# Attention scores with a head's two query parts in the two partition halves, and a new sequence of the mixer's steps, in a hybrid decoder layer

## The chip, the cores and the metric

The kernel runs on one core of one Trainium2 chip. The metric is the device time of one execution in microseconds. A core has five engines that each work through a fixed list of instructions in order and wait for each other through semaphores: TensorE (PE in the profile, its weight loads PEld), VectorE (DVE), ScalarE (ACT), GpSimd (POOL) and SyncE (SP), which issues the transfers from memory.

## The reference

One decoder layer on 512 tokens of width 1024, in float32. Three parts follow each other: a SwiGLU half-step (inner width 2816), a token mixer, a second SwiGLU half-step with a gated embedding behind it. The change is inside the mixer, in the attention scores:

```python
z = h @ w_in[i]
zq, zk, zv, zc, zg = [z[..., offs[j]:offs[j + 1]] for j in range(len(SPLIT_SIZES))]
q = rmsnorm(zq.reshape(B, S, N_Q_HEADS, HEAD_DIM), q_norm[i])
k = rmsnorm(zk.reshape(B, S, N_KV_HEADS, HEAD_DIM), k_norm[i])
q = partial_rope(q, cos, sin)
k = partial_rope(k, cos, sin)
a = sliding_window_attention(q, k, v, sinks[i]) @ attn_proj[i]
...
s = jnp.einsum('bnqhgd,bnkhd->bnhgqk', qb, kb, preferred_element_type=jnp.float32) * scale
valid = (delta >= 0) & (delta < WINDOW) & (kpos >= 0)
...
merged = jax.nn.sigmoid(ga) * a + jax.nn.sigmoid(gb) * c
x = x + merged @ w_out[i]
```

There are 16 query heads and 2 key heads of 64 channels, and 8 query heads share a key head. Tokens stand in 4 blocks of 128. The queries of a block see the keys of their own block and of the block before; block 0 has no block before it. Beside the attention (a) the mixer has a convolution branch (c): a gated projection, a causal depthwise convolution with 31 taps over 1024 channels, a layer norm, a projection. Two further projections (ga, gb) gate the two branches.

## The kernel before, in words

**Number format.** Every large product is done with operands in a rounded float32 format (F32R). To keep the precision, an operand x is split into a high part xh = round(x), written by ScalarE, and a low part xl = x - xh, written by DVE (`split_into`, L681). A product of two split operands is three products: wh·xl, wl·xh, wh·xh (`mm3`, L708). All weights are split in this way as they arrive, in pieces of 128x1024: the transfer fills raw, ScalarE writes whi, DVE or POOL writes wlo (the remainder).

**What sets the order of the work.** The code does not issue instructions directly. `record` (L652) records every operation with its operands; a planner (`simulate`, `plan`) plays the five engines through with a cost for each operation, and gives each operation an engine slot and each tile a buffer. The order on PE begins with the sequence in which groups of products were recorded; a group whose inputs are late may be overtaken by up to nine others, and five passes feed the result back. On the other engines the operation with the earliest due time goes first. Remainders of some weights are "flex": the planner puts them on DVE or on POOL. The finished lists are fixed in the program. PSUM gives 8 buffers.

**The mixer's steps.** `ORDER` (L40) is a string that gives the sequence in which the mixer's steps are recorded: K (keys and values), Q0, Q1 (queries of head groups 0 and 1), a0 to a7 and b0 to b7 (the two halves of the convolution's gated projection, for eight channel blocks; the convolution of a channel block follows its b step), A, E and V (scores, softmax, values; A0 to A3 are group 0 and blocks 0 to 3, A4 to A7 group 1), g and h (the gates ga and gb), p (the attention's output projection), L (the convolution's layer norm), e (the embedding's product). After them come the convolution's projection (cp) and the output (wo).

**Scores.** `scores(g, t)` (L1259) handles the eight heads of group g in token block t as four pairs j. In the tiles a pair lies in the partitions: head j, which uses key head 0, in partitions 0 to 63, and head j + 8, which uses key head 1, in 64 to 127. PE transposes the queries (qTp), they are split into qT_h and qT_l with all 128 partitions, and `mm3` multiplies them with kz. The tile kz (high and low) holds for key head 0 the keys in partitions 0 to 63 and zeros in the others, for key head 1 the other way round; so one product with both key heads side by side gives both heads of the pair. Per pair there are three products of 512 columns (two key heads, two blocks of 128 keys), or of 256 columns in block 0. Four POOL memsets write the zeros.

**Around it.** Behind the scores ScalarE copies the part of the own block, DVE puts in the earlier block by a predicated copy, finds the maximum, and ScalarE takes the exponentials. `values(g, t)` (L1314) transposes the probabilities (pT), splits them (p_h, p_l) and multiplies them with the values (o). `conv(c)` (L1133) runs the taps of five channel blocks on DVE (tiles cz, 29 steps each) and of three on ScalarE (ct) and POOL (y).

Of the kernel before, what the change touches and what calls it, by code (L numbers as in the profile page):

```python
# [9 lines left out]
F32 = mybir.dt.float32  # L10
F32R = mybir.dt.float32r
I32 = mybir.dt.int32
AF = mybir.ActivationFunctionType
ALU = mybir.AluOpType
AX = mybir.AxisListType

P = 128
# [8 lines left out]
HD = 64  # L26
NPAIR = NH // 2
W = 128
# [9 lines left out]


ORDER = """  # L40
K0 a0 b0 a1 Q0 A0 b1 a3 a2 A1 b2 E0 E1 b3 A2 E2 a4 V0 A3 a5 E3 V1 b4 Q1 V2 b5
V3 A5 a7 A6 g5 h7 A4 E5 A7 E6 E4 V6 g3 a6 E7 g0 V5 b6 V4 g4 g6 V7 h1 g2 h4 b7
g1 p0 p2 g7 p3 L0 p4 h3 p7 h2 p5 p1 e0 e1 p6 h5 h0 h6
"""
POOLCH = (0, 2, 4)
WARM = 9
# [605 lines left out]
def record():  # L652
    nc = Program()

    def ps_tile(name):
        return nc.tile(name, [P, S], F32, "ps")
# [4 lines left out]
    def rtile(name):  # L661
        return nc.tile(name, [P, S], F32R, "a")

    def small(name, n):
        return nc.tile(name, [P, n], F32, "c")
# [15 lines left out]
    def split_into(hi, lo, src, scale=None, eng=nc.vector):  # L681
        if scale is None:
            nc.scalar.activation(hi, src, AF.Copy)
            eng.tensor_tensor(lo, src, hi.bitcast(F32), op=ALU.subtract)
        else:
            nc.scalar.activation(hi, src, AF.Copy, scale=scale)
            nc.vector.scalar_tensor_tensor(
                lo, src, scale, hi.bitcast(F32), op0=ALU.mult, op1=ALU.subtract
            )

    def split(name, src, scale=None):
        hi, lo = rtile(f"{name}_h"), rtile(f"{name}_l")
        split_into(hi, lo, src, scale)
        return hi, lo
# [13 lines left out]
    def mm3(ps, w, x, start, stop, first=1, skip=False):  # L708

        nc.tensor.matmul(ps, w[first], x[0], start=start, stop=False, skip_group_check=skip)  # L710
        nc.tensor.matmul(ps, w[1 - first], x[0], start=False, stop=False, skip_group_check=skip)
        nc.tensor.matmul(ps, w[0], x[1], start=False, stop=stop, skip_group_check=skip)
# [132 lines left out]
    x, h = [], []  # L845
# [248 lines left out]
    def next_norm(tag, gain):  # L1094
        h, ss = [], SumSq(f"{tag}_ss")

        def after(o):
            h.append(split(f"{tag}_h{o}", x[o], gain[:, o : o + 1]))
            ss.in_psum(x[o], KD)

        return h, ss, after

    h2, ss2, after = next_norm("mix", g_mix)
# [92 lines left out]


    kz = [nc.tile(f"kz{p}", [P, NKV, S], F32R, "k") for p in "hl"]
    for z in kz:
        nc.behind = next(o for o in reversed(nc.ops) if o.eng == "PE")  # L1200
        nc.gpsimd.memset(z.bitcast(F32)[HD:P, 0], 0.0)
        nc.gpsimd.memset(z.bitcast(F32)[0:HD, 1], 0.0)
        nc.behind = None


    vd = [nc.tile(f"v{t}", [P, 2, NKV, 2, HD], F32R, "a") for t in range(NT)]
# [3 lines left out]
    def keys_values():  # L1210
        pss = token_major("kv", "wkv", 0, 2, 4, 2 * P)
        norm2()
        k3s = []
        for t in range(NT):
            z = nc.tile(f"zk{t}", [P, NKV, HD], F32, "a")
            p4 = pss[t].rearrange("p (b d) -> p b d", d=HD)
            r = r2k[:, t : t + 1]
            nc.scalar.activation(z, p4[:, 0:2], AF.Copy, scale=r)
            nc.scalar.activation(vf[:, t], p4[:, 2:4], AF.Copy, scale=r)
            for hh in range(NKV):  # L1220
                split_into(vp[t][:, hh, hh], vp[t][:, hh, 1 - hh], p4[:, 2 + hh], scale=r)
            k3s.append(z)
        for t in range(NT - 1, 0, -1):
            nc.gpsimd.tensor_tensor(vf[:, t], vf[:, t], vf[:, t - 1], op=ALU.subtract)
            for hh in range(NKV):
                split_into(dv[t][:, hh, hh], dv[t][:, hh, 1 - hh], vf[:, t, hh], eng=nc.gpsimd)
        rk = heads_rsqrt("k", k3s, NKV, 1.0, True)
        for t, k3 in enumerate(k3s):
            nc.vector.tensor_tensor(k3, k3, rk[t].unsqueeze(2).broadcast_to([P, NKV, HD]), op=ALU.mult)
            rest = k3[:, :, 16:HD]  # L1230
            nc.gpsimd.tensor_tensor(rest, rest, gqk.unsqueeze(1).broadcast_to([P, NKV, HD - 16]), op=ALU.mult)
            rope(f"k{t}", k3, NKV, kcs, t)
        pt = ps_tile("kTp")
        with nc.group("kT"):
            for t, k3 in enumerate(k3s):
                nc.tensor.transpose(pt[:, t * P : (t + 1) * P], k3.rearrange("p h d -> p (h d)"), ident)
        halves = [slice(hh * HD, (hh + 1) * HD) for hh in range(2)]
        for hh in range(2):
            r = halves[hh]
            split_into(kz[0][r, hh], kz[1][r, hh], pt[r])  # L1240

    zq, rq = {}, {}

# [15 lines left out]
    def scores(g, t):  # L1259

        pt = ps_tile(f"qTp{g}_{t}")
        with nc.group(f"qT{g}_{t}"):
            for j in range(4):
                nc.tensor.transpose(pt[:, j * P : (j + 1) * P], zq[g, t][:, j * P : (j + 1) * P], ident)
        qT = split(f"qT{g}_{t}", pt)
        nb = 1 if t == 0 else 2  # L1270
        t0 = t + 1 - nb
        s = [nc.tile(f"s{g}_{t}_{i}", [P, 2, 2, W], F32, "a") for i in range(2)]
        m = small(f"m{g}_{t}", 8)
        for j in range(4):
            ps = ps_tile(f"sc{g}_{t}_{j}")
            ps4 = ps.rearrange("p (h c k) -> p h c k", h=2, c=2)
            with nc.group(f"sc{g}_{t}_{j}"):
                q = [qT[i][:, j * P : (j + 1) * P] for i in range(2)]
                kk = [kz[i][:, :, t0 * W : (t + 1) * W] for i in range(2)]
                mm3(ps4[:, :, 0:nb], q, kk, True, True)  # L1280
            sj = s[j // 2][:, j % 2]
            if t == 0:
                nc.vector.tensor_tensor(sj, ps4[:, :, 0], later, op=ALU.add)
            else:
                nc.scalar.copy(sj, ps4[:, :, 1])
                nc.vector.copy_predicated(sj, later.bitcast(I32), ps4[:, :, 0])
            if j % 2:
                mj = m[:, 2 * j - 2 : 2 * j + 2].rearrange("p (j h) -> p j h", h=2)
                nc.vector.tensor_reduce(mj, s[j // 2], axis=AX.X, op=ALU.max, negate=True)
        nc.vector.tensor_tensor(m, m, rq[g][t], op=ALU.mult)  # L1290
        nc.vector.tensor_tensor(m, m, sinks_n[:, 8 * g : 8 * g + 8], op=ALU.min)
        state[g, t] = s, m
# [68 lines left out]
    def norm2():  # L1361
        nonlocal rb2, r2k
        rr = mean_rstd("mix_n", ss2.accs, D)
        r2k = rr[1]
        rb2 = spread("mix_n", rr)
# [102 lines left out]
    h3, ss3, after = next_norm("f2", g_ffn2)  # L1468
    for o in range(KD):
        ps = proj(f"wo{o}", "wout", o, mg)  # L1470
# [4 lines left out]
    h4, ss4, after4 = next_norm("pg", g_gate)  # L1475
# [4 lines left out]
    for o in range(KD):  # L1480
        ps = proj(f"pg{o}", "wgate", o, h4)
# [140 lines left out]
```

## Time and profile before

| | |
|---|---|
| median of 3 runs | 1172.97 us (1172.74 to 1175.81) |
| profiled execution | 1174.18 us, span of the trace 1172.4 us |
| PE busy | 1161.6 us (99%), 6740 products |
| DVE busy | 973.4 us (83%) |
| ScalarE busy | 639.7 us (55%) |
| POOL busy | 456.2 us (39%) |
| mixer: first key product, first cp, first wo product | 354.0, 690.3, 733.8 us |
| score products | start from 422.8 to 533.5 us, 96 of them |

Tiles are named as in the program: ca and cb are the products of the steps a and b, sc the scores, o the values, q0b and q1b the query projections, wlo_... the weight remainders, sg the convolution's sigmoid gate, u its input, sga and sgb the gates, ln_... the convolution's layer norm, ple_... the embedding's norm. The whole program is issued by a helper, so nearly all rows carry line 1522, and operations are told apart by tile. A product's duration runs from its start to its modelled end, and products overlap; the rate is read from the starts.

### The profile page before, as it was taken

The page shows a single profiled execution, that of the slowest core. Times are in us where ns is not written, and L with a number is a line of the kernel's source. Part 1 is how long each engine was busy: PE and PEld are TensorE (multiplying, and loading weights), DVE is VectorE, ACT ScalarE, POOL GpSimd, SP SyncE. Part 2 cuts the span into 40 slices and gives each one's busy share as a digit, 9 for nine tenths or more (in the row PEclk, how much of TensorE's full clock was granted, in tenths as well). Part 3 has the DMA queues.
Part 4 walks back from the last instruction along what each step waited for, and adds up shares of the span by engine and source line. Part 5 has one row for each costly group of instructions (what it writes and reads, how often), then busy time and mean ns, then how long its engine had stood idle before and what let it go on. Part 6 is the DMA issues. An engine that isn't in the chain of part 4 may idle for free.

```text
span 1172.4 us, 17962 instructions
## 1 busy us (share of the span) xinstructions
PE 1161.6 (99%) x6740; PEld 1029.6 (88%) x6740; DVE 973.4 (83%) x1481; ACT 639.7 (55%) x1139; POOL 456.2 (39%) x418
## 2 busy tenths in 40 slices
PE   9999999999999999999999999999999999999998
PEld 7898899889988888878888888889988999899886
DVE  8995799679886898999999786678966997599885
ACT  8552455335545579979865573545541555245542
POOL 2430465033303987887898600104402440122000
PEclk9999999999999999999999999999999999999999
DMA  7422323342233221312223233332333223331331
GB/s 226 146 85 96 126 75 106 99 136 76 82 104 100 90 91 37 108 55 72 76 89 106 88 94 93 105 96 102 107 104 132 74 86 100 121 127 41 104 108 72
DMA packets 37815, 115.30 MB, mean 98 GB/s; under 512 B 4704, under 2 KB 9440, under 8 KB 37728
## 3 DMA queue, kind: packets, MB, share of 16 engines
q1 hardware_dynamic: 37584, 114.12, 31.0%
q8 instruction: 53, 0.87, 0.3%
q14 instruction: 34, 0.28, 0.1%
q10 hardware_dynamic: 144, 0.03, 0.0%
HBM read 112.04 MB, written 2.10 MB: 97 GB/s over the span
## 4 chain that ended last, share of the span: by engine, by line
PE 94%; ACT 2%; DVE 2%; POOL 1%; issue 1%; DMA 0%; SPq 0%; DVEq 0%; ACTq 0%
PE f_d L1522 20%; PE ap L1522 4%; PE ga L1522 4%; PE pg L1522 4%; PE cp L1522 4%; PE wo L1522 4%; PE ca L1522 3%; PE gb L1522 3%; PE cb L1522 3%; PE f_u L1522 2%; PE f_g L1522 2%; PE q1b L1522 2%; PE q0b L1522 2%; PE sc L1522 2%; PE f_u14b L1522 1%; PE f_u20b L1522 1%
## 5 line engine op out<-in xcount | busy, mean ns | idle before, releaser
L1522 POOL TENSOR_TENSOR f_s<-raw_wgu,raw_wgu 128x512 f32<-128x512 f32 x51 | 86.6, 1710 | 345.5 <-DMA raw_wgu<-in_wgu 115.6
L1522 POOL TENSOR_TENSOR y<-y,ct 128x507 f32<-128x507 f32 (+27 forms) x90 | 119.1, 1343 | 6.2 <-ACT ct L1522 4.6
L1522 ACT ACTIVATE whi_wgu<-raw_wgu 128x1024 fp32r<-128x1024 f32 (+1 forms) x93 | 76.2, 834 | 81.5 <-PE f_d L1522 29.5
L1522 DVE TENSOR_TENSOR wlo_wgu<-raw_wgu,whi_wgu 128x1024 fp32r<-128x1024 f32 (+1 forms) x93 | 105.1, 1140 | 7.8 <-ACT whi_wgu L1522 7.3
L1522 DVE SCALAR_TENSOR_TENSOR cz<-u,dww,cz 128x504 f32<-128x504 f32 (+25 forms) x145 | 104.7, 732 | 2.3
L1522 ACT ACTIVATE whi_wd<-raw_wd 128x1024 fp32r<-128x1024 f32 (+1 forms) x48 | 47.4, 987 | 103.9 <-PE f_d L1522 84.6
L1522 DVE TENSOR_TENSOR f_d<-f_d,f_n_rb 128x512 f32<-128x512 f32 x48 | 33.4, 697 | 75.8 <-PE f_d L1522 75.8
L1522 DVE TENSOR_TENSOR f_wl<-f_s,f_wh 128x512 fp32r<-128x512 f32 x72 | 71.4, 1012 | 1.5 <-ACT f_wh L1522 1.0
L1522 POOL TENSOR_TENSOR f_s<-raw_wgu,f_s 128x512 f32<-128x512 f32 x31 | 52.3, 1694 | 51.6 <-DVE f_us L1522 20.6
L1522 DVE TENSOR_TENSOR wlo_wgu<-f_s,whi_wgu 128x512 fp32r<-128x512 f32 x80 | 66.3, 863 | 6.0 <-ACT whi_wgu L1522 5.8
L1522 ACT ACTIVATE whi_wgu<-f_s 128x512 fp32r<-128x512 f32 x80 | 46.6, 625 | 32.4 <-PE f_d L1522 8.9
L1522 ACT ACTIVATE ct<-u,dww 128x505 f32<-128x505 f32 (+28 forms) x90 | 58.2, 701 | 2.2 <-DVE u L1522 2.1
L1522 ACT ACTIVATE f_wh<-f_s 128x512 fp32r<-128x512 f32 x72 | 43.6, 626 | 26.6 <-DVE f_s L1522 12.9
L1522 POOL TENSOR_TENSOR f_s<-f_s,raw_wgu 128x512 f32<-128x512 f32 x31 | 49.2, 1594 | 20.8 <-DVE f_s L1522 6.0
L1522 DVE TENSOR_TENSOR wlo_wd<-raw_wd,whi_wd 128x1024 fp32r<-128x1024 f32 (+1 forms) x48 | 54.1, 1128 | 3.8 <-ACT whi_wd L1522 3.6
L1522 ACT ACTIVATE f_gs<-f_gs 128x512 f32<-128x512 f32 x44 | 27.6, 629 | 34.8 <-DVE f_gs L1522 34.4
L1522 POOL TENSOR_TENSOR f_t<-x 128x256 f32<-128x256 f32 x8 | 6.5, 807 | 86.8 <-DVE x L1522 81.6
L1522 DVE SCALAR_TENSOR_TENSOR x<-f_d,x 128x512 f32<-128x512 f32 x48 | 32.9, 689 | 1.4
L1522 DVE TENSOR_TENSOR f_s<-raw_wgu,raw_wgu 128x512 f32<-128x512 f32 x25 | 32.9, 1319 | 0.0
L1522 ACT ACTIVATE s<-s,m,q_r 128x128 f32<-128x128 f32 x64 | 31.0, 491 | 0.5 <-DVE m L1522 0.4
L1522 ACT ACTIVATE whi_wzc<-raw_wzc 128x1024 fp32r<-128x1024 f32 x16 | 17.0, 1061 | 22.3 <-issue 8.4
L1522 ACT ACTIVATE whi_wzg<-raw_wzg 128x1024 fp32r<-128x1024 f32 x16 | 17.1, 1069 | 16.9 <-PE ga L1522 5.0
(1621 smaller groups left out, 4525.3 us busy)
## 6 DMA issues: line engine op xcount, KB each, us to landing
raw_wgu<-in_wgu SPq DMA_DIRECT2D x80, 512.0 KB, 3.7
raw_wd<-in_wd SPq DMA_DIRECT2D x32, 512.0 KB, 3.5
raw_wzc<-in_wzc SPq DMA_DIRECT2D x16, 512.0 KB, 3.6
raw_wzg<-in_wzg SPq DMA_DIRECT2D x16, 512.0 KB, 3.6
raw_wd<-in_wd SPq DMA_DIRECT2D x16, 384.0 KB, 3.1
raw_wgu<-in_wgu SPq DMA_DIRECT2D x32, 128.0 KB, 2.9
raw_wq<-in_wq SPq DMA_DIRECT2D x8, 512.0 KB, 3.6
raw_wap<-in_wap SPq DMA_DIRECT2D x8, 512.0 KB, 3.6
```

The costliest lines, as they stand in the source:

```text
L1522: getattr(engines[op.eng], op.what)(*a, **k)
```

## The change

In `scores` the split of the transposed queries is laid out in another way. For head hh of a pair there is one tile qT[hh]: in the head's own 64 partitions the high part, in the other 64 the low part of the same head. kz now holds, for each key head, the same keys in both halves. A product of qT[hh] with the high keys so gives (qh + ql)·kh, and a second one with the low keys gives (qh + ql)·kl. Per pair that is four products, two for each head, of 256 columns, or of 128 in block 0. The zeros and their memsets are gone; the keys take four ScalarE and four DVE instructions on 64 partitions for two and two; the queries of a step take two ScalarE and two DVE instructions on 64 partitions and 512 columns for one and one on 128 partitions. `ORDER` has the same steps in another sequence.

```diff
 ORDER = """
-K0 a0 b0 a1 Q0 A0 b1 a3 a2 A1 b2 E0 E1 b3 A2 E2 a4 V0 A3 a5 E3 V1 b4 Q1 V2 b5
-V3 A5 a7 A6 g5 h7 A4 E5 A7 E6 E4 V6 g3 a6 E7 g0 V5 b6 V4 g4 g6 V7 h1 g2 h4 b7
-g1 p0 p2 g7 p3 L0 p4 h3 p7 h2 p5 p1 e0 e1 p6 h5 h0 h6
+K0 a0 a1 b0 Q0 A0 a3 b1 E0 a2 A1 E1 b3 a5 A2 V1 a4 E2 b2 V0 A3 E3 b4 Q1 V2 A6
+h7 V3 E6 b5 a7 A5 g5 A4 E5 E4 A7 V5 V6 g3 g6 a6 b6 h1 V4 g4 E7 b7 g0 V7 h3 h4
+p0 g2 g1 h2 g7 p2 p3 h6 p5 p6 p1 L0 p4 h5 e0 e1 h0 p7
 """
...
     kz = [nc.tile(f"kz{p}", [P, NKV, S], F32R, "k") for p in "hl"]
-    for z in kz:
-        nc.behind = next(o for o in reversed(nc.ops) if o.eng == "PE")
-        nc.gpsimd.memset(z.bitcast(F32)[HD:P, 0], 0.0)
-        nc.gpsimd.memset(z.bitcast(F32)[0:HD, 1], 0.0)
-        nc.behind = None
+    mixer = next(o for o in reversed(nc.ops) if o.eng == "PE")
...
         for hh in range(2):
             r = halves[hh]
-            split_into(kz[0][r, hh], kz[1][r, hh], pt[r])
+            nc.behind = mixer
+            for to in (r, halves[1 - hh]):
+                nc.scalar.activation(kz[0][to, hh], pt[r], AF.Copy)
+            for to in (r, halves[1 - hh]):
+                nc.vector.tensor_tensor(kz[1][to, hh], pt[r], kz[0][r, hh].bitcast(F32), op=ALU.subtract)
+            nc.behind = None
...
-        qT = split(f"qT{g}_{t}", pt)
+
+        qT = [rtile(f"qT{g}_{t}_{hh}") for hh in range(2)]
+        for hh in range(2):
+            r, other = (slice(h * HD, (h + 1) * HD) for h in (hh, 1 - hh))
+            nc.scalar.activation(qT[hh][r], pt[r], AF.Copy)
+            nc.vector.tensor_tensor(qT[hh][other], pt[r], qT[hh][r].bitcast(F32), op=ALU.subtract)
...
             with nc.group(f"sc{g}_{t}_{j}"):
-                q = [qT[i][:, j * P : (j + 1) * P] for i in range(2)]
-                kk = [kz[i][:, :, t0 * W : (t + 1) * W] for i in range(2)]
-                mm3(ps4[:, :, 0:nb], q, kk, True, True)
+                for hh in range(2):
+                    for i in (1, 0):
+                        nc.tensor.matmul(
+                            ps[:, 2 * hh * W : (2 * hh + nb) * W], qT[hh][:, j * P : (j + 1) * P],
+                            kz[i][:, hh, t0 * W : (t + 1) * W], start=i == 1, stop=i == 0,
+                        )
```

PE has 32 products more (four for three in 32 pairs). In the planned lists the places below matter. In their names the digits behind a tile's letters are group, block, pair or half (sc1_0_0 is group 1, block 0, pair 0; qT1_0_1 the tile of half 1), and the number at the end is a buffer.

First place: the scores of head group 1. On PE before, from the transposes of block 1 to its first score:

```order
L1522 MATMUL qTp1_1_5515<-ident_72,zq1_1_5394 128x128 x4
L1522 MATMUL qTp1_2_5522<-ident_72,zq1_2_5401 128x128 x4
L1522 MATMUL o0_3_0_5532<-p0_3_0_h_5450,v2_4083 128x512
L1522 MATMUL o0_3_0_5532<-p0_3_0_l_5467,v2_4083 128x512
L1522 MATMUL o0_3_0_5532<-po0_3_0h_5465,v3_4091 128x512
L1522 MATMUL o0_3_0_5532<-po0_3_0l_5490,v3_4091 128x512
L1522 MATMUL o0_3_1_5540<-p0_3_1_h_5457,v2_4083 128x512
L1522 MATMUL o0_3_1_5540<-p0_3_1_l_5475,v2_4083 128x512
L1522 MATMUL o0_3_1_5540<-po0_3_1h_5505,v3_4091 128x512
L1522 MATMUL o0_3_1_5540<-po0_3_1l_5513,v3_4091 128x512
L1522 MATMUL sc1_1_0_5555<-kzh_4314,qT1_1_l_5546 128x512
```

Block 1 now has the 24 products of a gate (ga5) between its transposes and its scores, and it is block 0 that follows at once. On PE now, from the last scores of block 1 to those of block 0:

```order
L1531 MATMUL sc1_1_3_5770<-kzl_4328,qT1_1_1_5703 128x256
L1531 MATMUL sc1_1_3_5770<-kzh_4312,qT1_1_1_5703 128x256
L1531 MATMUL qTp1_0_5781<-ident_72,zq1_0_5440 128x128 x4
L1531 MATMUL qTp1_3_5794<-ident_72,zq1_3_5475 128x128 x4
L1531 MATMUL sc1_0_0_5807<-kzl_4328,qT1_0_0_5788 128x128
L1531 MATMUL sc1_0_0_5807<-kzh_4312,qT1_0_0_5788 128x128
L1531 MATMUL sc1_0_0_5807<-kzl_4328,qT1_0_1_5791 128x128
L1531 MATMUL sc1_0_0_5807<-kzh_4312,qT1_0_1_5791 128x128
```

Before, the transposes of blocks 0 and 3 of this group had a whole gate projection between them and their scores; now only block 3's four transposes stand there, and block 3's scores follow those of block 0. On DVE before, the splits of the place first shown:

```order
L1522 SCALAR_TENSOR_TENSOR cz3_4863<-u3_4854,dww_221,cz3_4863 128x484
L1522 SCALAR_TENSOR_TENSOR cz5_5283<-u5_5257,dww_221,cz5_5283 128x500
L1522 SCALAR_TENSOR_TENSOR cz3_4863<-u3_4854,dww_221,cz3_4863 128x483
L1522 SCALAR_TENSOR_TENSOR cz5_5283<-u5_5257,dww_221,cz5_5283 128x499
L1522 TENSOR_TENSOR of0_2_5441<-o0_2_1_5503,of0_2_5441 64x512
L1522 TENSOR_TENSOR qT1_1_l_5546<-qTp1_1_5515,qT1_1_h_5530 128x512
L1522 TENSOR_TENSOR qT1_2_l_5553<-qTp1_2_5522,qT1_2_h_5536 128x512
```

Conv steps (cz) and a value sum (of) stood ahead of the splits. On DVE now, those of blocks 0 and 3:

```order
L1531 SCALAR_TENSOR_TENSOR cz5_5332<-u5_5320,dww_221,cz5_5332 128x491
L1531 TENSOR_TENSOR wlo_wzg12_5774<-raw_wzg12_5568,whi_wzg12_5750 128x1024
L1531 COPY_PREDICATED s1_1_0_5767<-masks_210,sc1_1_0_5743 128x256
L1531 COPY_PREDICATED s1_1_0_5767<-masks_210,sc1_1_1_5755 128x256
L1531 TENSOR_TENSOR qT1_0_0_5788<-qTp1_0_5781,qT1_0_0_5788 64x512
L1531 TENSOR_TENSOR qT1_0_1_5791<-qTp1_0_5781,qT1_0_1_5791 64x512
L1531 COPY_PREDICATED s1_1_1_5779<-masks_210,sc1_1_2_5762 128x256
L1531 COPY_PREDICATED s1_1_1_5779<-masks_210,sc1_1_3_5770 128x256
L1531 TENSOR_TENSOR qT1_3_0_5804<-qTp1_3_5794,qT1_3_0_5804 64x512
L1531 TENSOR_TENSOR qT1_3_1_5809<-qTp1_3_5794,qT1_3_1_5809 64x512
```

The splits come in two halves each, between the predicated copies of block 1.

Second place: the values of group 0, block 0. On PE before, from the transposes of its probabilities (pT0_0_0, pT0_0_1) on:

```order
L1522 MATMUL pT0_0_0_4899<-ident_72,s0_0_1_4661 128x128 x2
L1522 MATMUL pT0_0_1_4906<-ident_72,s0_0_0_4644 128x128 x2
L1522 MATMUL pT0_0_1_4906<-ident_72,s0_0_1_4661 128x128 x2
L1522 MATMUL qTp0_3_4913<-ident_72,zq0_3_4522 128x128 x4
L1522 MATMUL ca5_4921<-mix_h0_h_3680,wlo_wzc10_4825 128x512
L1522 MATMUL ca5_4921<-mix_h0_h_3680,whi_wzc10_4810 128x512
```

The 24 products of ca5 stood before the values of this block. On PE now:

```order
L1531 MATMUL pT0_0_0_5105<-ident_72,s0_0_1_4668 128x128 x2
L1531 MATMUL pT0_0_1_5115<-ident_72,s0_0_0_4642 128x128 x2
L1531 MATMUL pT0_0_1_5115<-ident_72,s0_0_1_4668 128x128 x2
L1531 MATMUL sc0_3_0_5122<-kzl_4328,qT0_3_0_4933 128x256
L1531 MATMUL sc0_3_0_5122<-kzh_4312,qT0_3_0_4933 128x256
L1531 MATMUL sc0_3_0_5122<-kzl_4328,qT0_3_1_4937 128x256
L1531 MATMUL sc0_3_0_5122<-kzh_4312,qT0_3_1_4937 128x256
L1531 MATMUL sc0_3_1_5129<-kzl_4328,qT0_3_0_4933 128x256
L1531 MATMUL sc0_3_1_5129<-kzh_4312,qT0_3_0_4933 128x256
L1531 MATMUL sc0_3_1_5129<-kzl_4328,qT0_3_1_4937 128x256
L1531 MATMUL sc0_3_1_5129<-kzh_4312,qT0_3_1_4937 128x256
L1531 MATMUL o0_0_0_5152<-p0_0_0_h_5137,v0_4069 128x512
```

Eight scores of block 3 are all that now stands between; ahead of these rows are the gate projection cb4 and four value products (o0_1_1). On DVE now, from the sigmoid gate of that projection (sg4) to the splits that the values read (p0_0_0_l, p0_0_1_l):

```order
L1531 TENSOR_TENSOR sg4_5099<-cb4_5031,mix_n_rb_4183 128x512
L1531 SCALAR_TENSOR_TENSOR cz3_4814<-u3_4792,dww_221,cz3_4814 128x494
L1531 SCALAR_TENSOR_TENSOR cz3_4814<-u3_4792,dww_221,cz3_4814 128x493
L1531 TENSOR_TENSOR wlo_wq4_5132<-raw_wq4_4914,whi_wq4_5108 128x1024
L1531 SCALAR_TENSOR_TENSOR cz3_4814<-u3_4792,dww_221,cz3_4814 128x492
L1531 TENSOR_TENSOR p0_0_0_l_5145<-pT0_0_0_5105,p0_0_0_h_5137 128x512
L1531 TENSOR_TENSOR of0_1_5036<-o0_1_1_5094,of0_1_5036 64x512
L1531 TENSOR_TENSOR p0_0_1_l_5157<-pT0_0_1_5115,p0_0_1_h_5143 128x512
```

Before, the two splits followed a maximum and four predicated copies; a weight remainder and conv steps stand there now.

Third place: the end of the convolution. On DVE before, the last rows up to the sum that the layer norm's mean product reads (ln_s_l):

```order
L1522 SCALAR_TENSOR_TENSOR y7_6611<-u7_6596,dww_221,cz7_6602 128x511
L1522 TENSOR_TENSOR sga7_6717<-ap7_6857,sga7_6717 128x512
L1522 TENSOR_TENSOR ln_acc1_5965<-ln_acc1_5965,y7_6611 128x512
L1522 TENSOR_TENSOR wlo_wap1_6925<-raw_wap1_6792,whi_wap1_6909 128x1024
L1522 TENSOR_TENSOR sgb2_6946<-gb2_6906,mix_n_rb_4183 128x512
L1522 TENSOR_TENSOR wlo_wple0_6957<-raw_wple0_6842,whi_wple0_6948 128x1024
L1522 TENSOR_TENSOR ln_s_l_6979<-ln_acc0_6920,ln_s_h_6974 128x512
```

Behind the gate product that ln_s_l follows here (gb2), PE had two projections before the mean product. On DVE now:

```order
L1531 SCALAR_TENSOR_TENSOR y7_6895<-u7_6435,dww_221,cz7_6479 128x511
L1531 TENSOR_TENSOR wlo_wap6_6929<-raw_wap6_6798,whi_wap6_6918 128x1024
L1531 TENSOR_TENSOR ln_acc1_5415<-ln_acc1_5415,y7_6895 128x512
L1531 TENSOR_TENSOR sgb6_6959<-gb6_6911,mix_n_rb_4183 128x512
L1531 TENSOR_TENSOR wlo_wap1_6970<-raw_wap1_6845,whi_wap1_6961 128x1024
L1531 TENSOR_TENSOR sga5_5752<-ap5_6956,sga5_5752 128x512
L1531 TENSOR_TENSOR wlo_wap4_7007<-raw_wap4_6891,whi_wap4_6999 128x1024
L1531 TENSOR_TENSOR sga6_6004<-ap6_6994,sga6_6004 128x512
L1531 TENSOR_TENSOR ln_s_l_7039<-ln_acc0_6987,ln_s_h_7028 128x512
```

Behind ap6, which ln_s_l now follows, PE has one projection before the mean product. From the last gate projection of the convolution (cb7, of step b7) to the mean product PE now has 14 projections, eight transposes and eight value products; before it had eleven projections. DVE's list in the same stretch has 86 rows where it had 58: 48 conv steps for 30, 11 weight remainders for 10, and 27 other rows for 18. Counted from the mixer's norm to ln_s_l, DVE has ten instructions more for queries and keys, one gate product more and two weight remainders more, POOL two remainders and four memsets less.

## The prediction

> **What bounds the kernel now.** Read first: the page's busy shares, then its chain of waits, then the list of what TensorE (PE) waited for.
>
> ```profile
> span 1172.4 us, 17962 instructions
> PE 1161.6 (99%) x6740; PEld 1029.6 (88%) x6740; DVE 973.4 (83%) x1481; ACT 639.7 (55%) x1139; POOL 456.2 (39%) x418
> PE 94%; ACT 2%; DVE 2%; POOL 1%; issue 1%; DMA 0%; SPq 0%; DVEq 0%; ACTq 0%
> ```
>
> ```profile
> PE sc L1522 <- DVE qT_l L1522: 2.0, 1, 2.0
> ...
> PE ple_sp L1522 <- DVE ple_dgl L1522: 0.6, 1, 0.6
> ...
> PE kTp L1522 <- POOL zk L1522: 0.2, 1, 0.2
> ```
>
> PE is the bound: its work and a few waits make the time. In the mixer these three waits (2.8 us) are all; no transfer is among them. So the change is worth the PE time it takes out, plus or minus waits. VectorE (DVE) is the engine that could make new ones. Busy time by stretch (columns: stretch, length, then busy us of PE, PEld, DVE, ACT, POOL):
>
> ```profile
> 400.00:480.00 80.00, 80.00 (x378) 66.72 (x377) 72.12 (x129) 67.73 (x147) 67.49 (x80) 1.00 0.24 74
> 480.00:600.00 120.00, 117.99 (x557) 98.16 (x556) 116.91 (x188) 101.77 (x213) 103.23 (x121) 1.00 0.24 75
> 600.00:645.00 45.00, 45.00 (x200) 37.29 (x199) 43.67 (x52) 24.10 (x35) 40.46 (x29) 1.00 0.34 104
> 366.00:645.00 279.00, 276.77 (x1282) 229.95 (x1282) 258.83 (x433) 213.66 (x438) 232.93 (x268) 1.00 0.27 82
> ```
>
> **Term A: scores of blocks 1 to 3.** Durations of products overlap, so starts are what counts.
>
> ```profile
> 430.17 0.39 PE L1522 MATMUL sc<-kzh,qT_l 128*128 128x512 f32 x1
> ...
> 432.88 0.39 PE L1522 MATMUL cb<-mix_h_h,wlo_wzc 128*128 128x512 f32 x1
> ```
>
> ```profile
> 422.82 0.28 PE L1522 MATMUL sc<-kzh,qT_l 128*128 128x256 f32 x1
> ...
> 424.25 0.60 PE L1522 MATMUL qTp<-ident,zq 128*128 128x128 f32 x4
> ```
>
> Twelve products of 512 columns took 432.88 - 430.17 = 2.71 us, 0.226 each; twelve of 256 took 1.43, 0.119 each. Blocks 1 to 3 of either group (six steps) now run 16 products of 256: 16 x 0.119 = 1.90 for 2.71. Saved: 6 x 0.81 = **4.8 us**.
>
> **Term B: block 0.** It has one key block, so its 16 products are 128 columns wide, and took 1.43 as twelve of 256. No product of this type is that narrow in the trace. Below: half of 0.119, so 16 x 0.06 = 0.95, a gain of 0.5 a step. Above: the startup products, full float32, 128 columns, 18 records in 4.21 us, 0.23 each; 16 x 0.23 = 3.7, a loss of 2.25 a step. Nearest are the transposes, 128 columns with a load for each:
>
> ```profile
> 1.11 4.21 PE L1522 MATMUL warm<-ones 128*128 128x128 f32 x18 [1.11 <-DVE ones L1522]
> ...
> 501.93 1.04 PE L1522 MATMUL qTp<-ident,zq 128*128 128x128 f32 x8
> 502.72 0.48 PE L1522 MATMUL o<-p_h,v 128*128 128x512 f32 x1
> ...
> 506.80 0.50 PE L1522 MATMUL sc<-kzh,qT_l 128*128 128x512 f32 x1 [2.01 <-DVE qT_l L1522]
> ```
>
> Eight took 0.79, 0.10 each; with the slower product behind them (0.32 to the next start instead of 0.23) 0.11. I take 0.11: 16 x 0.11 = 1.76, two steps lose **0.66 us**; ends -1.0 and +4.5.
>
> [...]
>
> **Term C: waits that go.** The 2.0 us came because only eight value products stood between the transposes of block 1 and its scores. In the new sequence a whole projection (ga, 5.4 us) does. The 0.6 of ple_sp goes: two output products now stand ahead of it. Together **2.6 us**; kTp keeps its 0.2.
>
> **Term D: waits that come.** Two places have less cover than any in the old order. First, group 1, block 0: between its transposes and its scores stand only the four transposes of block 3, 0.4 us. Durations of the steps between:
>
> ```profile
> L1522 ACT ACTIVATE kzh<-kTp x2: 572/584/596, 390.4 to 391.0; 64x512 fp32r<-64x512 f32 x2
> L1522 DVE TENSOR_TENSOR kzl<-kTp,kzh x2: 673/684/695, 391.7 to 392.4; 64x512 fp32r<-64x512 f32 x2
> L1522 POOL MEMSET kzh<- x2: 520/520/521, 393.0 to 393.5; 64x512 f32 x2
> ...
> L1522 DVE TENSOR_TENSOR qT_l<-qTp,qT_h x8: 675/678/691, 419.9 to 527.5; 128x512 fp32r<-128x512 f32 x8
> L1522 DVE COPY_PREDICATED s<-masks,sc x24: 432/441/472, 433.1 to 534.6; 128x256 f32<-128x256 int32 x24
> ```
>
> At least one half on ScalarE and one on DVE: 0.58 + 0.68 - 0.4 = 0.9. At most the old case: the transposes of block 1 ended at 502.3 and its scores began at 506.8, 4.5 - 0.4 = 4.1. The order shows two predicated copies on DVE ahead of two halves where five conv steps stood before: 0.58 + 2 x 0.44 + 2 x 0.68 - 0.4 = 2.4 us. Block 3's scores follow: its splits come two copies and two halves later on DVE, 2 x 0.44 + 2 x 0.68 = 2.24, while PE has block 0's 1.76 and two products, 2.0. That adds 0.3: **2.7 us** in all.
>
> Second, group 0, block 0: its values follow its own transposes after eight scores. From the end of the gate projection cb4 PE has 0.91 + 0.76 + 8 x 0.119 + 0.23 = 2.9 us until it needs p0_0_0_l. DVE has, in the order's rows, a gate product (0.68), three conv steps, a weight remainder (wlo_wq) and the split itself:
>
> ```profile
> L1522 DVE SCALAR_TENSOR_TENSOR cz<-u,dww,cz 128x504 f32<-128x504 f32 (+25 forms) x145 | 104.7, 732 | 2.3
> ...
> L1522 DVE TENSOR_TENSOR wlo_wap<-raw_wap,whi_wap 128x1024 fp32r<-128x1024 f32 x7 | 11.9, 1716 | 0.0
> L1522 DVE TENSOR_TENSOR wlo_wzg<-raw_wzg,whi_wzg 128x1024 fp32r<-128x1024 f32 x6 | 11.0, 1835 | 0.1
> ...
> L1522 DVE TENSOR_TENSOR wlo_wq<-raw_wq,whi_wq 128x1024 fp32r<-128x1024 f32 x5 | 7.0, 1400 | 1.4 <-ACT whi_wq L1522 1.3
> ...
> L1522 DVE TENSOR_TENSOR ln_acc<-ln_acc,y 128x512 f32<-128x512 f32 x3 | 4.8, 1586 | 0.0
> ```
>
> 0.68 + 3 x 0.73 + 1.40 + 0.68 = 5.0, so **2.1 us** of wait. Below: nothing, if DVE is ahead there. Above 3.0: the second half's split stands two rows later (1.37 against 0.93 of PE work), and a remainder can take 1.84. Behind the waiting product on PE stand two scores, two transpositions and a gate projection; ScalarE's copies of those scores and the next conv channel wait for them in turn, but both have PE's 21.8 us of q1b behind them to catch up.
>
> **What costs nothing.** The keys' extra ScalarE and DVE instructions (two each) and the four memsets that go (0.52 each) lie at 390 to 395; the first score reads the keys at 422.8, with the 21.8 us of q0b between:
>
> ```profile
> 389.81 21.80 PE q0b L1522 x96
> ```
>
>  Without that cover two splits would cost 2.5 us. Eight more ScalarE halves (0.58) fall on an engine with 65 us to spare between 366 and 645. SP issues the same transfers in another sequence, past each other but past nothing else; its queue waits for free buffers, and PE waited for none of it. POOL loses two weight remainders as well.
>
> **The sum.** -4.8 + 0.7 - 2.6 + 4.8 = -1.9 us, or -2.0 with a second decimal kept (4.84, 0.66). The profiled execution took 1174.18 (span 1172.4 and 1.8 around it), 1.2 above the median of 1172.97; the difference is taken from the median: **1171.0 us**.
>
> **Rivals.** *Cheap narrow products and half the waits.* With B at -1.0 and D at 2.4: -4.8 - 1.0 - 2.6 + 2.4 = -6.0, 1167.0. For it: starts 0.226 and 0.119 apart for 512 and 256 columns, nearly in proportion; against it, the transposes' 0.10. *Narrow products in several passes:* B at +4.5, so -2.0 - 0.7 + 4.5 = +1.8, 1174.8; only the startup rows speak for it, and they are full float32.
>
> *DVE becomes the bound of the mixer (the other side).* The convolution's mean product (ln_mb) needs DVE's ln_s_l. Up to there the order has ten more halves or splits (6.8), one more gate product (0.7) and two more weight remainders (3.4): 10.9 us.
>
> ```profile
> 592.71 0.39 PE L1522 MATMUL ga<-mix_h_h,wlo_wzg 128*128 128x512 f32 x1
> ...
> 652.56 0.39 PE L1522 MATMUL ln_mb<-ln_s_h,mean_r 128*128 128x512 f32 x1
> ```
>
> ```profile
> 593.63 0.68 DVE L1522 TENSOR_TENSOR sg<-cb,mix_n_rb 128x512 f32<-128x512 f32 x1
> ...
> 644.16 0.68 DVE L1522 TENSOR_TENSOR ln_s_l<-ln_acc,ln_s_h 128x512 fp32r<-128x512 f32 x1
> ```
>
> Old slack: 652.56 - 644.84 = 7.7. If DVE keeps its 20 us of idle since 366, ln_s_l ends at 366 + 258.8 + 10.9 + 20 = 655.7; PE would ask at 652.56 - 4.8 + 0.7 - 2.0 + 4.8 = 651.3: 4.4 late, and in all 4.4 - 1.3 - 0.6 = +2.5, **1175.5**. It decides once DVE idles more than 15 us before ln_s_l. Against it: the last gate projection now stands earlier. Behind it PE has 14 projections of 5.45 (q0b above: 96 products in 21.80, so 24 take 5.45), eight transposes and eight value products, 78.9 us, ahead of ln_mb; DVE has 48 conv steps (35.1), 11 remainders (19.6), two sums (3.2) and 25 smaller (20 of 0.68, one of 1.04, four conv ends of 2.4 together): 74.9. The same count before gives 52.7 and took 51.2 (593.63 to 644.84). Margin some 4 us, less than before, so a late DVE is possible.
>
> **How the numbers follow.** Forecast 0.50, cheap narrow products 0.28, several passes 0.08, DVE 0.14. All terms at their good ends give -7.5 (1165.5), at their bad ends +4.2 (1177.2); leaving 2 in 10 out, the range is 1166.0 to 1176.0; the forecast's own is 1168.5 to 1174.0. About 0.3% (3.5 us) is what a measurement of this kernel can tell from no change. Faster by more: the cheap case and a sixth of the forecast, 0.36. Slower by more: half of the DVE case and the edges of the others, 0.13. Within: 0.51.
>
> **What would show it.** Right: sixteen scores of 256 columns in 1.9 us; those of 128 in about 1.8; PE's waits listing qT for group 1 blocks 0 and 3, and p_l for group 0 block 0, with 2 to 3 us each; ln_mb without a wait. Wrong: narrow scores 0.06 or 0.23 apart; ln_mb waiting for ln_s_l; waits at the other six score steps, each of which has a projection of 5.4 us as cover.

## The result, and the profile after

The changed kernel takes 1191.4 us, the kernel before 1173.0: a ratio of 1.0154 (95% interval 1.0141 to 1.0166), 18 us slower. 1171.0 was predicted, with 1166 to 1176 as the range.

The page's first rows of the changed kernel, and the row of TensorE's granted clock in 40 slices:

```profile
span 1189.6 us, 18042 instructions
PE 1168.5 (98%) x6772; PEld 1034.2 (87%) x6772; DVE 983.3 (83%) x1492; ACT 645.5 (54%) x1147; POOL 449.5 (38%) x413
...
PEclk9999999999999998999999999999999999999999
```

PE's busy time is 6.9 us more than before, though its work is some 4 us less: in this profile a busy us is not always a us at full clock (0.92 on the mean from 400 to 480 us, below). The slice with an 8 in the clock's row (446 to 476) is in group 0's attention. Of the list of what PE waited for, the rows that are new:

```profile
PE pT L1531 <- DVE u L1531: 3.9, 1, 3.9
PE o L1531 <- DVE p_l L1531: 2.3, 1, 2.3
PE qTp L1531 <- DVE s L1531: 1.7, 1, 1.7
PE sc L1531 <- DVE qT L1531: 1.3, 4, 0.4
PE qTp L1531 <- DVE q_y L1531: 1.2, 1, 1.2
...
PE cp L1531 <- ACT cv_h L1531: 0.9, 2, 0.8
...
PE qTp L1531 <- DVE y L1531: 0.6, 1, 0.6
```

Two of the stretches that were shown of before (length, then PE, PEld, DVE, ACT, POOL busy, and behind these the granted clock):

```profile
400.00:480.00 80.00, 71.70 (x336) 59.67 (x335) 74.63 (x132) 62.41 (x134) 59.21 (x75) 0.92 0.21 66
480.00:600.00 120.00, 117.16 (x567) 98.53 (x566) 109.04 (x182) 98.01 (x211) 88.98 (x113) 0.98 0.24 74
```

PE idles 8.3 us in the first stretch, where it had no idle time, and the clock there is 0.92. Followed along PE's list, the loss has one place above all. The marks are the first score product, the first product of the second group's query projection (q1b, behind group 0's attention) and the layer norm's mean product (ln_mb). After:

```profile
422.46 0.22 PE L1531 MATMUL sc<-kzl,qT 128*128 128x128 f32 x1
...
485.30 0.39 PE L1531 MATMUL q1b<-whi_wq,mix_h_l 128*128 128x512 f32 x1
...
666.49 0.39 PE L1531 MATMUL ln_mb<-ln_s_h,mean_r 128*128 128x512 f32 x1
```

Before, q1b:

```profile
471.38 0.47 PE L1522 MATMUL q1b<-whi_wq,mix_h_l 128*128 128x512 f32 x1
```

From the first score to q1b it was 48.6 us before (422.82 to 471.38) and is 62.8 now: 14.3 us more, though the scores between the marks are 2.1 us less work (four transposes more stand there, about 0.4). From q1b to ln_mb it is 181.2 in both, so the 2.1 us that the second group's scores save there, and the old wait of 2.0 that is gone, did not come either. The rest, with ScalarE's cv_h late for the convolution's output projections (0.9 us) and weight remainders late in the second feed-forward part, adds some 3 us.

How the 14 us come about, in rows of the timeline (start, length; [idle before <- what ended it]). First the longest wait:

```profile
446.56 0.39 PE L1531 MATMUL cb<-mix_h_l,whi_wzc 128*128 128x512 f32 x1
...
447.48 0.69 DVE L1531 TENSOR_TENSOR sg<-cb,mix_n_rb 128x512 f32<-128x512 f32 x1
...
448.04 1.04 ACT L1531 ACTIVATE whi_wzc<-raw_wzc 128x1024 fp32r<-128x1024 f32 x1
...
449.10 1.28 ACT L1531 ACT_TABLE_LOAD   x1
...
450.39 0.63 ACT L1531 ACTIVATE sg<-sg 128x512 f32<-128x512 f32 x1
...
451.15 1.27 POOL L1531 TENSOR_TENSOR sg<-sg,mix_n_rb 128x512 f32<-128x512 f32 x1
...
453.44 0.68 DVE L1531 TENSOR_TENSOR u<-ca,sg 128x512 f32<-128x512 f32 x1
...
454.17 1.12 PE L1531 MATMUL pT<-ident,s 128*128 128x128 f32 x4 [3.92 <-DVE u L1531]
...
455.94 0.63 PE L1531 MATMUL ca<-mix_h_l,whi_wzc 128*128 128x512 f32 x1
456.37 0.63 PE L1531 MATMUL ca<-mix_h_h,wlo_wzc 128*128 128x512 f32 x1
```

The transposes pT do not read u. What they need is a PSUM buffer: in the kernel's plan the one that holds ca, which u is the last to read. From the end of the gate projection (cb) to u there are 7 us: DVE's product, then on ScalarE the softmax's exponentials (until 448.04), a weight's rounding, a table load and only then the sigmoid, then POOL, then u. And behind the wait the projection's products of 512 columns start 0.43 us apart in place of 0.226. The granted clock by the microsecond:

```profile
452.00:453.00 1.00, 0.00 (x0) 1.00 0.68 254
453.00:454.00 1.00, 0.00 (x0) 0.50 0.50 201
...
459.00:460.00 1.00, 1.00 (x4) 0.58 0.00 0
460.00:461.00 1.00, 1.00 (x6) 1.00 0.08 16
```

The column behind PE's busy time is the granted clock: 1.00, then 0.50 from 453.0 to 459.8, then 1.00 again. Of these 6.8 us 1.2 lie inside the wait and 5.7 are work at half the rate: the wait cost 3.9 us and then another 2.8.

**The whole balance**, of the profiled executions (1189.6 against 1172.4, 17.2 us): PE's work -4.2; its waits by the two lists 15.4 against 5.4, so +10.0; the clock +7.7, the half of the 15.3 us that PE worked at 0.50 in the mixer, where before it had 1.00 (the mean clock over the span, 0.992 against 0.999, also holds low clock inside waits and behind the last product, which costs nothing more). That is 13.5; 3.7 us are not placed by this count (each wait is followed by a slow start of 0.1 to 0.3 us, and gaps under 0.15 us are in no list).

### The profile page after: what moved, and what is told of

Read it like the earlier page. It is cut to its first block, busy times and chain, and to the rows that moved or that the text cites. A ratio compares the mean times of both kernels' runs of the same rounds, so it can differ in the third digit from the quotient of the medians.

```text
span 1189.6 us, 18042 instructions
## 1 busy us (share of the span) xinstructions
PE 1168.5 (98%) x6772; PEld 1034.2 (87%) x6772; DVE 983.3 (83%) x1492; ACT 645.5 (54%) x1147; POOL 449.5 (38%) x413
## 4 chain that ended last, share of the span: by engine, by line
PE 86%; DVE 7%; ACT 5%; issue 2%; DMA 0%; POOL 0%; DVEq 0%; ACTq 0%; POOLq 0%
PE f_d L1531 20%; PE pg L1531 4%; PE wo L1531 4%; PE cp L1531 3%; PE ga L1531 3%; PE ap L1531 3%; PE gb L1531 3%; PE cb L1531 3%; PE ca L1531 2%; PE f_u L1531 2%; PE f_g L1531 2%; PE q1b L1531 2%; DVE cz L1531 2%; DVE wlo_wgu L1531 1%; PE f_u14b L1531 1%
## 5 line engine op out<-in xcount | busy, mean ns | idle before, releaser
L1531 DVE TENSOR_TENSOR wlo_wgu<-raw_wgu,whi_wgu 128x1024 fp32r<-128x1024 f32 (+1 forms) x93 | 107.9, 1172 | 6.1 <-ACT whi_wgu L1531 6.0
L1531 DVE SCALAR_TENSOR_TENSOR cz<-u,dww,cz 128x510 f32<-128x510 f32 (+27 forms) x145 | 103.0, 732 | 1.5
L1531 ACT ACTIVATE ct<-u,dww 128x509 f32<-128x509 f32 (+28 forms) x90 | 58.0, 701 | 1.7 <-DVE u L1531 1.5
```

The source lines that it names most:

```text
L1531: getattr(engines[op.eng], op.what)(*a, **k)
```

## The experiments

Theories. **S**: the new sequence makes the waits. **F** (later **H**): the new form makes them, by its eight more halves on ScalarE and on DVE. **L**: the lists that the planner makes for the new form. **N**: the faster products only arrive sooner at buffers that are not free. **D**: DVE's load. **C**: chains through ScalarE, POOL and DVE.

### The two parts apart

Form alone: the old string ORDER in the changed kernel. Sequence alone: the new string in the kernel before.

```diff
 form alone (after.py):      ORDER = """ K0 a0 b0 a1 Q0 A0 b1 a3 a2 A1 b2 E0 E1 ... """
 sequence alone (before.py): ORDER = """ K0 a0 a1 b0 Q0 A0 a3 b1 E0 a2 A1 E1 b3 ... """
```

> The new form of the scores alone, in the old sequence of steps. TensorE has 4.2 us less to do than before (24 pairs of blocks 1 to 3 save 4.8, block 0 loses 0.66). Theory S (the sequence makes the waits): the waits stay near the 2.8 us of before, so about 1169 us, ratio to before 0.996, granted clock 1.00 in the mixer. Theory F (the form makes them: eight more halves on each of ScalarE and DVE hold PSUM buffers longer): several us of new waits and clock loss, 1176 us or more.

> The new sequence of steps with the old form of the scores. TensorE has the work of before. Theory S: the waits for PSUM buffers in group 0 (3.9, 2.3, 1.2, 0.6 us in the changed kernel) and about as much clock loss are there too: 1185 us or more. Theory F: most of them are gone, 1175 us or less.

Measured: form alone 1184.1 us, ratio 1.0076 (1.0050 to 1.0102); sequence alone 1179.5, ratio 1.0048 (1.0030 to 1.0065). Both lose, the form more, and 1.24% of the 1.54% is the sum of the two. S is refuted as the whole (the new sequence alone is 1179.5 us, not 1185 or more): the form in the old sequence has waits that neither kernel had there:

```profile
PE sc L1531 <- DVE sga L1531: 2.7, 1, 2.7
PE qTp L1531 <- DVE q_rs L1531: 1.8, 1, 1.8
PE o L1531 <- POOL po_1h L1531: 1.2, 1, 1.2
```

### The form in lists that are not replanned

Each kernel's instructions on each engine follow from the planner's run. Here the old form was planned, and only the instructions of queries, keys and scores were exchanged when the lists were written out.

```diff
 for op in sorted(prog.ops, ...):
+    if writes kz: two copies / two subtractions for one (no memset)
+    if writes qT: halves, 64 partitions each, in the new layout
+    if writes sc: four products of the new form for six
     getattr(engines[op.eng], op.what)(*a, **k)
```

> The kernel before, its lists instruction for instruction, with the new form put in at the places of the old one: two copies and two subtractions of 64 x 512 where one of each of 128 x 512 stood, four products a head pair where six stood, the keys' parts in both halves, no memsets. Nothing else moves. Theory L (the lists that the planner makes for the new form cost the time, with the sequence that it picks on TensorE): the old lists keep their cover, TensorE saves 4.2 us, the 2.0 us wait before the scores of group 1 grows by the second half's 0.58 + 0.68 - 0.68, so about 1170 us, ratio 0.997 or less. Theory H (the added halves themselves hold PSUM buffers too long): new waits of 0.6 to 1.3 us at most of the eight steps and clock loss, 1177 us or more.

> The kernel with the new sequence and the old form, its lists instruction for instruction, with the new form put in at the places of the old one. Against the changed kernel only the planner's rearrangement of the other work is taken away; against the kernel with the sequence alone (1179.5 us) only the form is added. Theory L: about 1176 us (1179.5 less 4.2, plus a little waiting). Theory H: 1184 us or more, near the changed kernel's 1191.

Measured: 1184.8, ratio 1.0087 (1.0071 to 1.0104), and 1194.0, ratio 1.0161 (1.0142 to 1.0181). The first agrees with the form alone, the second with the changed kernel, each within its interval. L falls: how the planner rearranged the rest is not what costs the time. The form costs about 1%, on either sequence. One thing is not quite the form's own in these two runs: the second copy stands in ScalarE's list where the old subtraction stood in time, up to 1.0 us behind the first, and some of their loss may be that.

### What in the form costs it

In the changed kernel's lists, one copy and one subtraction of 128 partitions a step in place of two and two of 64:

> The changed kernel's lists, with one copy on ScalarE and one subtraction on DVE, each of 128 x 512, for the two and two of 64 x 512 in each of the eight query splits (so the scores are sums of other parts than the reference's; products, buffers and sequence are as in the changed kernel). That takes 0.58 us off ScalarE and 0.68 off DVE a step. Theory F (the added halves make the buffers late): the four waits of group 0 shrink from 8.3 us to under 3, time under 1180. Theory S: they stay above 6 us, time 1187 to 1191.

Measured: 1186.0, ratio 1.0100 (1.0083 to 1.0116): about a third of the loss goes. The two longest waits stand as they were, 3.9 and 2.3 us. Neither F nor S as I had put them.

Then each part by itself, in before's lists: only the new products (the splits as before), only the halves on both engines, only those on DVE, only those on ScalarE.

```diff
 only the halves:
+            if op writes qT:
+                for r in (slice(0, HD), slice(HD, P)):
+                    the same instruction on partitions r
```

> Before's lists with the new products (four of 256 columns a head pair, 128 in block 0) and the keys in both halves, but with the query splits left as they were, one copy and one subtraction of 128 x 512 each (so the scores are sums of other parts than the reference's). Only TensorE's saving, 4.2 us, without the added halves. Theory H (the added halves cost the time): 1169 to 1171 us, ratio 0.997 or less, waits near 3 us. Theory N (scores made faster only arrive sooner at the PSUM buffers that ScalarE and DVE must empty, so the saving turns into waiting): 1173 to 1176 us, waits of 5 us or more at the score steps.

> The kernel before with every query split written as two copies and two subtractions of 64 partitions; same values, same products. Only the added halves: 8 x 0.58 us on ScalarE, 8 x 0.68 on DVE. Theory H: +12 us or more over before (1186), since the form with them lost 10 while saving 4.2. Theory N: +3 to +6 (1177 to 1180).

> The kernel before with only the subtraction on DVE in two halves. DVE is 97 per cent busy from 480 to 600, ScalarE 85: if DVE is the engine that matters, this has most of what both halves cost, 70 per cent or more; if it is the length of the chain copy, subtraction, product, about half.

> The kernel before with only the copy on ScalarE in two halves. If DVE is the engine that matters, under 30 per cent of what both halves cost, 1174 to 1177 us; if it is the length of the chain, about half.

Measured against before: new products alone 1.0024 (1.0013 to 1.0035); both halves 1.0045 (1.0031 to 1.0059); DVE's alone 1.0045 (1.0032 to 1.0057); ScalarE's alone 1.0024 (1.0014 to 1.0033). The halves cost 5.3 us, not the 12 of H; DVE's alone cost as much as both, ScalarE's half of it. Products and halves together are 0.69%, the whole form in these lists 0.87.

The first number is the one that matters most. PE has 4.2 us less to do, nothing else has more but two copies and two subtractions of the keys, and the kernel is no faster but 2.8 us slower. In its profiled execution the 2.0 us wait of before is gone, and these have come:

```profile
PE sc L1538 <- DVE of L1580: 1.7, 2, 1.1
PE qTp L1580 <- DVE q_rs L1580: 1.3, 1, 1.3
...
PE sc L1538 <- DVE s L1580: 0.4, 1, 0.4
```

None of these is a wait for an operand of the product: of and s are what DVE makes of the PSUM buffers of earlier products, q_rs is DVE's work beside them. So N holds: most of what PE saves it spends at the next buffer. In this execution the stretch from the first score to the projection ca behind the last one is 110.1 us where before took 110.9, so 0.9 of the 4.2 us is left in it; its span is 0.5 us longer all the same, for delays in the feed-forward parts, of which 0.6 us stands before 75 us. Why the median lies 2.8 us above before's is not shown by this trace.

### Is it DVE's load?

58 of the convolution's steps on DVE were left out between 395 and 560 us in the changed kernel's lists, and 60 in before's lists with the new form.

```diff
+            if op is a conv step on DVE and 395.0 < op.start < 560.0:
+                taps += 1
+                if taps % 3: continue
```

> The changed kernel's lists without 58 of the convolution's 0.73 us steps on DVE between 395 and 560 us (two of three left out, 42 us; the convolution's values are then others than the reference's). Everything else stands as it was. Theory D (DVE's late instructions hold the PSUM buffers, and the clock falls behind the waits): the waits in the mixer go from 13.5 us to under 4, the clock stays at 1.00, and the time is 1171 to 1175. Rival C (chains through ScalarE and POOL hold them, DVE only stands at their end): the 3.9 us wait behind the gate's sigmoid and most of the 2.3 stay, time 1182 or more.

> Before's lists with the new form, and 60 of the convolution's steps on DVE between 395 and 560 us left out in the same way (44 us; the convolution's values are others than the reference's). Theory D: the form at last shows its 4.2 us, 1167 to 1170, waits in the mixer under 2 us. Rival C: at least half of the 10 us that this kernel lost with all steps stays, 1178 or more.

Measured: 1187.7, ratio 1.0123 (1.0106 to 1.0140), and 1177.9, ratio 1.0045 (1.0030 to 1.0060). From 400 to 480 DVE was now busy for 59 of 80 us, and the waits were still there:

```profile
400.00:480.00 80.00, 73.03 (x356) 61.25 (x355) 59.01 (x105) 66.43 (x140) 62.70 (x80) 0.96 0.23 73
```

```profile
PE pT L1536 <- DVE u L1536: 4.2, 1, 4.2
PE o L1536 <- DVE p_l L1536: 2.3, 1, 2.3
PE qTp L1536 <- DVE s L1536: 1.7, 1, 1.7
```

D is refuted for these three, 8.2 us; the 1.2 us wait at 425 did go, and about half of the form's loss in the old lists. What would hold the long ones is length of chains (C): in the timeline above ScalarE comes to the sigmoid at 450.4, whatever DVE does (for u this is read from the rows; no run moved that sigmoid). The 2.3 us wait for p_l has the same look:

```profile
470.76 0.82 PE L1531 MATMUL pT<-ident,s 128*128 128x128 f32 x6
...
470.42 1.04 ACT L1531 ACTIVATE whi_wq<-raw_wq 128x1024 fp32r<-128x1024 f32 x1
...
471.48 1.28 ACT L1531 ACT_TABLE_LOAD   x1
...
472.77 0.63 ACT L1531 ACTIVATE sg<-sg 128x512 f32<-128x512 f32 x1
...
473.43 0.60 ACT L1531 ACTIVATE p_h<-pT 128x512 fp32r<-128x512 f32 x1
...
474.87 0.50 PE L1531 MATMUL o<-p_h,v 128*128 128x512 f32 x1 [2.34 <-DVE p_l L1531]
```

The transposes are done at 471.6; ScalarE's copy p_h starts at 473.4, behind a rounding of 1.04, a table load of 1.28 and a sigmoid of 0.63 that this product does not wait for. The product reads p_h and not p_l: in the kernel's plan it writes the buffer of the transposes, which p_l is the last to read, so the end of this wait too is a buffer's.

### The named instructions out of the way

```diff
 ScalarE:  +p_h (0,0)  +p_h (0,1)  table load  sg4  whi_wq4  of  -p_h (0,0)  -p_h (0,1)
 DVE:      ... p_l (0,0)  of  p_l (0,1)  +wlo_wq4 ...        +u2  wlo_wzc9  -u2
```

> The changed kernel with a few rows moved on ScalarE and DVE, nothing left out: the two copies of block 0's probabilities (p_h) ahead of a weight rounding, a table load and the gate's sigmoid on ScalarE, the remainder of that weight on DVE behind the two splits; and at the other place the product u ahead of a weight remainder on DVE. Theory C (instructions that PE does not wait for stand ahead, in ScalarE's and DVE's order, of those that empty its buffers): the 2.3 us wait for p_l goes, the 3.9 us wait for u becomes 2.9, one or two windows of low clock of 3.4 us (1.7 us lost each) go with the first: 1191.4 less 3.3 less 1.7 or 3.4, 1185 to 1187. Rival (the waits only move to the next buffer): 1189 or more.

Measured: 1193.7, ratio 1.0152 (1.0137 to 1.0167): no gain.

```profile
PE pT L1550 <- DVE u L1550: 2.9, 1, 2.9
PE sc L1550 <- DVE of L1550: 2.4, 1, 2.4
PE qTp L1550 <- DVE s L1550: 1.7, 1, 1.7
PE qTp L1550 <- DVE q_y L1550: 1.2, 1, 1.2
...
PE o L1550 <- DVE p_l L1550: 0.8, 1, 0.8
```

The two waits did what was expected of them, 3.9 to 2.9 and 2.3 to 0.8; but 2.4 us came at the very next score products, for a buffer that holds an output product (of) whose copy now stands behind the moved ones. The rival's time is what was measured: this reordering gains nothing. The new wait is one that the move itself made, so it is not shown that no other one would.

### The form in a third sequence

```diff
+K0 a0 a1 Q0 b1 b0 a3 A0 a2 b3 A1 E1 a5 V1 a4 E0 A2 E2 b2 A3 V0 E3 Q1 b4 V2 A6
+V3 b5 A4 h7 E6 A5 V6 a7 A7 E4 E5 V5 E7 g6 h1 a6 b6 h3 h5 V7 h4 V4 g3 g2 g5 b7
+g0 g1 g4 p2 p4 p5 h6 g7 L0 p6 p0 h0 h2 p1 e0 e1 p3 p7
```

> The changed form of the scores in another sequence of steps, one in which each gate projection and softmax stands so that the PSUM buffers of the steps ahead of it have longer to be emptied. If the form's 4.2 us can be had at all, waits in the mixer of 3 us or less, none over 2, clock 1.00: 1168 to 1172, ratio 0.997 or less. If the form's added instructions make some waits whatever the sequence (theory H), 1176 or more.

Measured: 1180.6, ratio 1.0047 (1.0034 to 1.0061). Two thirds of the change's loss come back by sequence alone, with waits of 1.6 us at most; faster than before it is not, as theory H had it. No version tried beats the kernel before.

### The clock

Does a short wait lower the clock because narrow products stand beside it? In outline:

```diff
+ block 0: ps[:, 2*hh*W : (2*hh+2)*W], kz[:, hh, 0:2*W]   # 256 columns, the second half not read
```

> The changed kernel's lists, with the 32 score products of block 0 made 256 columns wide (the second key block's columns are written and not read): 0.119 us apart for 0.112, 0.1 us a step. [...] If only waits count, the time stays at 1191 to 1192 and the clock at 426 to 429 stays 0.50.

Measured: 1189.2, ratio 1.0129 (1.0114 to 1.0144), and the clock at 424 to 428 is 1.00 where the changed kernel has 0.71, after a wait of 1.1 us for 1.2. That looked like a yes. But in the kernel with moved rows, whose lists up to there are those of the changed kernel, with narrow products and a wait of 1.2, it is 1.00 from 424 to 428 too. Same work, same wait, and the clock fell in one and not in the other. What differs in the traces is where the stretches of half clock lie. In every kernel that has several, they begin whole multiples of 3.413 us apart (in the changed one at 425.70, 453.01, 476.90 and 538.34: 8, 7 and 18 times, 112.64 us in 33; with the moved rows at 452.4, 476.3 and 537.8: 7 and 18 times). With the time before them divided into windows of this length, one window of the changed kernel holds both the narrow products and most of the wait, while the moved rows have them in two (length, PE's busy time, the clock; the changed kernel first):

```profile
422.29:425.70 3.41, 2.26 (x18) 1.00 0.43 154
425.70:429.11 3.41, 3.16 (x9) 0.50 0.50 141
```

```profile
421.70:425.11 3.41, 3.21 (x22) 1.00 0.51 154
425.11:428.53 3.42, 1.87 (x10) 1.00 0.26 60
```

Sorted by such windows, the attention (395 to 560 us) of all sixteen kernels speaks for the width. The four windows at full clock with 14 or more products of 128 columns and 0.88 to 1.23 us without work were all followed by half clock; of the 19 with at most eight such products and 0.88 to 1.33 us without work none was, the one of the wide version (422.65 to 426.06, 1.00 us) among them. This is a sorting after the fact, and the windows themselves are read from the spacing, as an estimate: no run held their place and the waits and changed the width alone. What the 2 us of this run come from is only in part placed: its waits by the list are those of the changed kernel (15.5 us against 15.4), but the mixer has three portions of half clock, not five.

## Why the prediction was wrong

**A (-4.8) was right as work, wrong as time.** Sixteen products took 1.9 us, 0.12 each:

```profile
433.49 0.28 PE L1531 MATMUL sc<-kzl,qT 128*128 128x256 f32 x1
...
435.28 0.28 PE L1531 MATMUL sc<-kzh,qT 128*128 128x256 f32 x1
435.40 0.40 PE L1531 MATMUL ca<-mix_h_h,wlo_wzc 128*128 128x512 f32 x1
```

The step failed in "the change is worth the PE time it takes out, plus or minus waits": with the products alone, none of the 4.2 us came in the time of the kernel, and 2.8 were lost.

**B (+0.66)** was right: in block 0 the products of 128 columns start 0.11 apart. The rival of several passes, 4.5 us, and that of cheap narrow products, -1.0, are both out.

```profile
423.25 0.27 PE L1531 MATMUL sc<-kzl,qT 128*128 128x128 f32 x1
...
424.48 0.27 PE L1531 MATMUL sc<-kzh,qT 128*128 128x128 f32 x1
```

**C (-2.6)**: both waits went, and 0.9 at cp came with the new sequence, in a place that I had not looked at.

**D (+4.8)** came out near in size, for reasons that were partly others. D2, "nothing, if DVE is ahead there", 2.1 us: measured 2.3, but with two thirds of DVE's conv steps left out it is still 2.3, since ScalarE's copy was late and not DVE: the size came out right by luck. D1, 2.7 us: 1.7 for a buffer ahead of block 3's transposes and three of 0.4 for the halves, 2.8.

**The step that failed** is the sentence on where waits come: "Two places have less cover than any in the old order". The count looked from each product to what makes its operands. It did not look at the eight PSUM buffers: who reads the one that a product is about to write, and how late. Of the new waits in the attention, 3.9 (u), 1.7 (s), 1.2 (q_y, beside which DVE reads block 0's first score buffer) and 0.6 (y, the last to read a convolution channel's accumulator, which lies in PSUM too), 7.4 us, are of that kind. Terms C and D together made the waits 2.2 us longer (-2.6 and +4.8); by the two lists they are 10.0 us longer. The profile before had the hint: DVE busy for 116.9 of 120 us from 480 to 600, ScalarE and POOL for over 100, and yet PE with one wait only, of 2.0 us. I read that row as three engines with some slack each; after the run with the products alone it looks like a plan whose buffers came free just in time.

**What costs nothing** was wrong for the halves: that ScalarE has "65 us to spare" there counts busy time, not the place in its queue. ScalarE's alone cost 2.8 us, DVE's alone 5.3, as much as its 8 x 0.68 us with nothing hidden.

**The clock** was in no term. Five portions of half clock in the mixer, 3.4 us each, cost 7.7 us beside the waits, over 40% of the loss.

**The rival on the slow side** (DVE bounds the mixer, the mean product ln_mb late) had the right engine among the suspects and the wrong place: ln_mb did not wait; it was 13.9 us late because PE was.

## What to carry to other kernels

An engine without waits may still be paced by those that empty its buffers. Here, with one of these busy for 97% of the stretch and two for some 85%, 4.2 us of work taken off TensorE made the kernel no faster. So ask of each product not only when its operands are ready but when the buffer that it writes was last read, and by what chain. An instruction added to that chain can cost its whole length, as DVE's halves did (5.3 us for eight of 0.68), however much idle time its engine has on the average. And price a TensorE wait with the half clock that may follow it: in these kernels it followed each wait of 2.3 us or more, for 3.4 or 6.8 us, and some of the shorter ones.

## What the runs showed of the hardware

**A wait costs TensorE clock, in portions.** In the profiled executions of all sixteen kernels, the granted clock behind waits in the mixer was either 1.00 or 0.50, never between for longer than a slice, and the low stretches were 3.4 or 6.8 us long: 1.7 or 3.4 us lost, less what falls inside the wait. All 14 waits of 2.3 us or more were followed by one (in the changed kernel the 3.9 us by 6.8 us at 0.50, the 2.3 by 3.4). Of 20 between 1.2 and 2.1 us 9 were (one more began at low clock, in a stretch that lies behind waits of 0.85 and 0.38 among narrow products); among those that were not are the 2.0 us wait of before and one of 2.1. Of 14 between 0.9 and 1.2 none was by itself (behind one, the clock fell in a second wait that followed). By the windows of 3.413 us that the section on the clock works out it sorts better: among those at full clock and with at most eight narrow products, 14 of 14 with 1.76 us or more without work were followed by half clock, 6 of 17 with 1.38 to 1.73, and none of the 19 with 0.88 to 1.33. In the changed kernel the windows with 2.76 and 1.38 us without work stand ahead of half clock, those with 1.62 and 0.96 ahead of 1.00. The length of the one wait does not decide by itself: in the pair above one of 1.2 us lowered the clock and its twin did not.

**A table load stands in line.** Where exponentials and sigmoids alternate, these traces have a table load on ScalarE in between, 1.28 us each. The changed kernel has 16 of them and the kernel before 18, so their number is not the matter; but the one at 449.1 and the one at 471.5 stand in the chains of the two longest waits.
